# Encoder block on Trainium2: order and queues of the second MLP pass' operand loads, and place of the down passes' first operand

## The chip, the cores and the metric

One NeuronCore of a Trainium2 chip runs the whole program. The time is device microseconds of one execution; the kernel before is given by the median of three runs, and the profile is of one more execution.

## The reference

A transformer block over one sequence: 16 meta tokens are put ahead of the tokens, attention and a Fourier mix run side by side on one input projection, then comes an MLP with squared ReLU, and the final norm drops the meta tokens. All is float32. The change touches the MLP alone.

```python
D_MODEL = 1024; SEQ = 2048; DEPTH = 1; D_FF = 4 * D_MODEL
...
for i in range(DEPTH):
    hn = rms_norm(h, g_mix[i])
    proj = hn @ w_in[i]
    ...
    mixed = jnp.concatenate([rms_norm(attn, g_attn_out[i]), rms_norm(four, g_fourier_out[i])], axis=-1)
    h = h + mixed @ w_out[i]
    m = rms_norm(h, g_mlp[i])
    h = h + jnp.square(jax.nn.relu(m @ w_up[i])) @ w_down[i]
return rms_norm(h, g_final)[:, N_META:]
```

## The kernel before, in words

The MLP takes about the last 1,260 us of 2293 and runs in two passes (p = 0 and 1), each over 1024 tokens. A pass is `up_pass` (eight weight groups g of 512 columns of w_up) and then `down_pass` (four groups). Every product of two matrices is made in seven "forms" of Strassen's scheme, in the order `ORDER = "1265734"`; each form multiplies one sum or difference of quarter matrices by another and is added into one or two quarters of the result. Since the matrices are float32 and TensorE works on rounded parts, each operand is split into a high part (a cast on ScalarE, L70) and a low part (a subtraction on VectorE, L71), and `mm3` makes high x high (L80), high x low (L81) and low x high (L82). A form of the up pass is 24 matmuls, 12 for each half q; one of the down pass is 48, 12 for each token tile t, k = 0..3, where k = 0, 1 use the operand's half h = 0 and k = 2, 3 its half h = 1.

Names, which the profile's rows carry:

- `bf`: the activations' operand of an up form (2 MB, high and low part). For pass 1 all seven were worked out during pass 0 and lie in DRAM as `f_d`. Lines 1603 to 1612 make their tiles and load them: six in the pool `bfb`, form 7 in the tile `e0`. The tiles `e0` and `e1` (pool `ey`) hold residual rows `hs` (t = 0..3 and 4..7) while a down pass runs, and other things between.
- `R`: two raw tiles of 1 MB, w_up's 512 columns of one group. `up_weights` (L1119) makes from them the weight operands `wuh`, `wul` of the seven forms, with sums `us` on VectorE (L1138, L1139, L1142, L1144); there is a ring of three pairs of tiles (`wu_tile`, `WU_BUFS = 3`). Pass 1's first two weight operands are made in pass 0's down pass from their own loads `we` (L1413).
- `ux`, `uy`: PSUM results of up forms; `p` copies (L1246, ScalarE) and `c` sums (L1257, VectorE, then relu and square on ScalarE, L1212 and L1213) take them out; `keep` (L1219) writes c and their sums s to DRAM as `s_d`, which the down pass reads as `a`.
- `dx`, `dy`: PSUM results of down forms, added to `hs` on VectorE (L1485). The operands are `ah`, `al` (from `a`) and `bh`, `bl` (from `d`, w_down).
- Pass 0's last down group ends each token tile with the final norm: `ers` on GpSimd (L1444), scaling on VectorE (L1450) and ScalarE (L1451), and stores `out_dram<-hs` on GpSimd's queue (L1454).

Each engine, and SyncE (SP) as a DMA queue, runs its instructions strictly in the order in which they stand; an instruction that waits for a semaphore holds all behind it. The order on each engine comes from the order of the code's calls and a scheduler that moves DMAs ahead. Seven loads of pass 1's forms, R's loads and the writes `s_d` all stand on SP. `first_down` (L1279) loads and splits the down pass' first operand: `up_pass` steps it in its last group (L1237), where R's tiles are free, and it splits half h = 0, then h = 1, of a and b.

Of the kernel before, what the change touches and what calls it, by code (L numbers as in the profile page):

```python
# [11 lines left out]
F32 = mybir.dt.float32  # L12
R32 = mybir.dt.float32r
# [6 lines left out]
P = 128  # L20
# [32 lines left out]
ORDER = "1265734"  # L53
# [3 lines left out]
def f32v(ap):  # L57
    return ap.bitcast(F32)
# [26 lines left out]
def ins_of(x):  # L85
    return getattr(x, "ins", x)
# [49 lines left out]
def encoder_block(ctx: ExitStack, tc: tile.TileContext, x, meta, w_in, w_f,  # L136
                  w_out, w_up, w_down, g_fin, g_cols, g_rows, c_id, c_rope, c_dft, c_even, c_odd, c_rem, out):
    nc = tc.nc
    split = Split(nc)
    x = x[0]  # L140
    out = out[0]
    w_in, w_out, w_up, w_down, w_f = w_in[0], w_out[0], w_up[0], w_down[0], w_f[0]
# [9 lines left out]
    ey = Lines(ctx.enter_context(tc.tile_pool(name="ey", bufs=1)), small)  # L152
# [7 lines left out]
    wu = Lines(tc.alloc_tile_pool(name="wu", bufs=1, side="right"), small)  # L160
# [40 lines left out]
    f_d = {n: dram.tile([P, 2, 4, 512], F32, name=f"f_d{n}") for n in ORDER}  # L201
# [390 lines left out]
    for j in range(LAST + 1):  # L592
# [16 lines left out]
        else:  # L609
# [14 lines left out]
            a = 0  # L624
# [399 lines left out]
    for k in range(NQ):  # L1024
        for h in range(2):
            raw = a_tile(f"wor{k}_{h}")
# [77 lines left out]
    s_d = [dram.tile([P, 7, 4, 512], F32, name=f"s_d{g}") for g in range(4)]  # L1104
# [9 lines left out]
    def wu_tile(name, tag, shape=(4, 256)):  # L1114
        return wup.tile([P, *shape], R32, name=name, tag=tag, bufs=WU_BUFS)
# [34 lines left out]
    BT = {}  # L1150
# [14 lines left out]
    def forms_ahead():  # L1165

        area = u_tile("lf", 1).rearrange("p k n -> p (k n)")
        items = list(itertools.product(range(4), range(2)))
        r, turn = {}, [0]

        def load(k, i):
            for n, b, kk in (("11", 2, k), ("21", 2, k + 4), ("12", 3, k), ("22", 3, k + 4)):
                r[n] = area[:, 256 * len(r):256 * len(r) + 256] if n not in r else r[n]
                nc.sync.dma_start(r[n], m_d[b][:, kk, i * 256:i * 256 + 256])

        def keep(name, src, k, i):
            t = area[:, 1024 + 512 * turn[0]:1536 + 512 * turn[0]].rearrange("p (e n) -> p e n", e=2)
            turn[0] ^= 1
            split(t[:, 0].bitcast(R32), t[:, 1].bitcast(R32), src)
            nc.sync.dma_start(f_d[name][:, :, k, i * 256:i * 256 + 256], t)  # L1180

        sub = lambda d, a, b: nc.vector.tensor_tensor(r[d], r[a], r[b], op=ALU.subtract)
        load(*items[0])
        yield
        for at, it in enumerate(items):
            keep("1", r["11"], *it)
            keep("2", r["21"], *it)
            yield
            sub("11", "12", "11")
            keep("5", r["11"], *it)  # L1190
            yield
            sub("11", "22", "11")
            keep("6", r["11"], *it)
            yield
            sub("12", "22", "12")
            keep("7", r["12"], *it)
            yield
            keep("3", r["22"], *it)
            yield
            sub("21", "21", "11")  # L1200
            keep("4", r["21"], *it)
            if at + 1 < len(items):
                load(*items[at + 1])
            yield

    def up_pass(p, sp, pc, UW, ready, first, hs, beside):

        def c_tile(name):
            return pc.tile([P, 512], F32, name=f"{name}_{p}", tag="c", bufs=11)

        def relu2(dst, src):
            nc.scalar.activation(dst, src, AF.Relu)  # L1212
            nc.scalar.square(dst, dst)  # L1213

        for g in range(8):
            X, Y, p1, u2, p5, C = ({} for _ in range(6))

            def keep(name, q, t):
                nc.sync.dma_start(s_d[g // 2][:, ORDER.index(name), 2 * (g % 2) + q], t)  # L1219

            for name in ORDER:
                hi, lo = ready.pop(0)
                m = BF[name]
                for q in range(2):
                    if name == "1":
                        X[q] = bank(f"ux_{p}_{g}_{q}")
                    elif name in "25":
                        Y[q] = ybank(f"uy{name}_{p}_{g}_{q}")
                    o = (Y if name in "253" else X)[q]
                    ps = slice(q * P, (q + 1) * P)  # L1230
                    for k in range(4):
                        mm3(nc, o, (hi[:, k, ps], lo[:, k, ps]), (m[0][k], m[1][k]),
                            name in "125" and k == 0, k == 3, True)
                w = next(UW, None)
                if w is not None:
                    ready.append(w)
                elif g == 7:  # L1237
                    next(first, None)
                    if name == "7":
                        load_h(p, 0, hs)  # L1240
                for q in range(2):
                    nm = f"{g}_{q}"
                    if name in "165":
                        d = p1 if name == "1" else u2 if name == "6" else p5
                        d[q] = pc.tile([P, 512], F32, name=f"p{name}_{p}_{nm}", tag="p", bufs=P_BUFS)
                        nc.scalar.copy(d[q], (Y if name == "5" else X)[q])  # L1246
                    elif name == "4":
                        C["21", q] = c = c_tile("c21_" + nm)
                        relu2(c, X[q])
                        keep("2", q, c)  # L1250
                        s4 = c_tile("s4_" + nm)
                        nc.vector.tensor_tensor(s4, c, C["s2", q], op=ALU.subtract)
                        keep("3", q, s4)
                    else:
                        f, a, b = {"2": ("11", Y, p1), "7": ("22", X, p5), "3": ("12", Y, u2)}[name]
                        C[f, q] = c = c_tile(f"c{f}_{nm}")
                        nc.vector.tensor_tensor(c, a[q], b[q], op=ALU.add)  # L1257
                        relu2(c, c)
                        if name != "3":
                            keep("1" if name == "2" else "4", q, c)  # L1260
                        else:
                            s1, s2, s3 = (c_tile(f"s{i}_{nm}") for i in (1, 2, 3))
                            nc.vector.tensor_tensor(s1, c, C["22", q], op=ALU.add)
                            keep("5", q, s1)
                            nc.vector.tensor_tensor(s2, s1, C["11", q], op=ALU.subtract)
                            keep("6", q, s2)
                            C["s2", q] = s2
                            nc.vector.tensor_tensor(s3, C["11", q], c, op=ALU.subtract)
                            keep("7", q, s3)
                next(beside, None)  # L1270
        drain(first, beside)
# [4 lines left out]
            (nc.gpsimd if i else nc.sync).dma_start(HS[:, t], h_d[8 * p + 4 * i + t])  # L1276
            hs.append(HS[:, t])

    def first_down(p, spr, FIRST, sp):  # L1279

        a = spr.tile([P, 4, 512], F32, name=f"a1_{p}", tag="R0")
        nc.sync.dma_start(a, s_d[0][:, 0])
        w = spr.tile([P, 4, 512], F32, name=f"d11_{p}", tag="R1")
        for h in range(2):
            nc.sync.dma_start(w[:, 2 * h:2 * h + 2], w_down[h * 512:h * 512 + 256, :512].rearrange("(p r) d -> r p d", r=P))
        yield
        for h in range(2):
            for x, r in (("a", a), ("b", w)):
                tags = ("us1", "us2") if h and x == "b" else ("wuh", "wul")
                hi, lo = ((wu_tile(f"{x}{e}1_{p}_{h}", t, (2, 512)) if t[0] == "w" else  # L1290
                           sp.tile([P, 2, 512], R32, name=f"{x}{e}1_{p}_{h}", tag=t)) for e, t in zip("hl", tags))
                split(hi, lo, r[:, 2 * h:2 * h + 2])
                FIRST.append((hi, lo))
                yield

    def down_pass(p, sp, FIRST, hs):

# [248 lines left out]
    sp = right("sp0")  # L1546
    UW = up_weights(0, sp, sp)
    ready = [next(UW), next(UW)]
# [40 lines left out]
    rest = later_forms()  # L1589
    next(rest)  # L1590
    pc = right("pc0")
    hs, FIRST = [], []
    up_pass(0, sp, pc, UW, ready, first_down(0, sp, FIRST, sp), hs, itertools.chain(rest, forms_ahead()))
    pc.release()
    bu.release()
    bf2.release()
# [3 lines left out]
    spr = left("spr1")  # L1600
    UW = up_weights(1, sp, spr)
    bfb = left("bfb")
    for name in ORDER:
        if name == "7":
            bf_tile(ey, name, tag="e0")
        else:
            bf_tile(bfb, name)
    nc.sync.dma_start(f32v(BT["1"]), f_d["1"])
    nc.sync.dma_start(f32v(BT["2"]), f_d["2"])
    ready.append(next(UW))  # L1610
    for name in "65734":
        nc.sync.dma_start(f32v(BT[name]), f_d[name])
    pc = right("pc1")
    hs, FIRST = [], []
    up_pass(1, sp, pc, UW, ready, first_down(1, spr, FIRST, sp), hs, iter(()))
    pc.release()
    bfb.release()
    spr.release()
# [103 lines left out]
```

## Time and profile before

| | |
|---|---|
| median of three runs | 2296.43 us (2295.06 to 2297.25) |
| the profiled execution | 2295.14 us |
| its span, first to last instruction | 2293.4 us |
| mean granted clock of TensorE | 0.994 |
| TensorE (PE) busy | 2242.5 us, 98% |
| VectorE (DVE) busy | 1692.7 us, 74% |
| ScalarE (ACT) busy | 1177.4 us, 51% |
| GpSimd (POOL) busy | 247.2 us, 11% |
| DMA queue of SP and the other hardware queue, share of 16 engines | 39.9% |
| DMA queue of GpSimd | 7.7% |

TensorE is busy for nearly the whole span; its idle time is some 50 us, and a change gains only what it takes from that idle time or from stretches at a lower clock. A row of a timeline has the start and duration in us, engine, line, operation, what it writes and reads, the shapes, and in brackets how long the engine was idle before it and what ended the wait. Consecutive matmuls overlap, so their pace is read from starts, not from durations.

### The profile page before, as it was taken

To read this page: it belongs to the slowest core of one execution; us is meant where nothing else is said; L and a number is where in the kernel's file an instruction comes from. 1 tells how busy PE (TensorE), PEld (TensorE's weight loads), DVE (VectorE), ACT (ScalarE), POOL (GpSimd) and SP (SyncE) were. 2 spreads that over 40 slices of the span, in tenths; PEclk is the share of its full clock that TensorE was granted. 3 is DMA by queue.
4 is the path that set the end of the run, shared out by engine and by line. 5 is a ranking of instruction groups with operands and counts; after the bars stand their busy time and mean duration, and the time that the engine had idled before them with its cause. 6 is when DMAs were issued, how large, how long until landed. Compare 5 with 4: busy or idle time off the path is not lost.

```text
span 2293.4 us, 28136 instructions
## 1 busy us (share of the span) xinstructions
PE 2242.5 (98%) x10238; PEld 1775.1 (77%) x10238; DVE 1692.7 (74%) x2250; ACT 1177.4 (51%) x1997; POOL 247.2 (11%) x285
## 2 busy tenths in 40 slices
PE   9999999999999999999999999999789999899998
PEld 7888986766666666678888878888678888688887
DVE  6435589999998998887776579779555656596795
ACT  6443356656555666677555544334345555443343
POOL 2212120013222022010000010000200000100000
PEclk9999999999999999999999999999899999999999
DMA  6333252133343523366767675543574445764442
GB/s 204 87 105 87 66 164 71 51 120 100 115 137 120 204 87 119 123 262 234 237 227 234 235 276 176 172 129 119 198 302 151 154 149 187 299 201 158 129 138 83
DMA packets 191787, 367.41 MB, mean 160 GB/s; under 512 B 15760, under 2 KB 74768, under 8 KB 189984
## 3 DMA queue, kind: packets, MB, share of 16 engines
q1 hardware_dynamic: 171040, 310.08, 39.9%
q0 software_dynamic: 20464, 55.27, 7.7%
q8 instruction: 80, 1.31, 0.2%
q14 instruction: 59, 0.48, 0.1%
q10 hardware_dynamic: 144, 0.26, 0.0%
HBM read 236.28 MB, written 129.27 MB: 159 GB/s over the span
## 4 chain that ended last, share of the span: by engine, by line
PE 79%; DVE 8%; DMA 6%; ACT 3%; issue 2%; POOL 1%; SPq 1%; POOLq 0%; DVEq 0%; ACTq 0%
PE o L849 6%; PE dx L80 5%; PE dx L82 5%; PE dx L81 5%; PE dy L82 4%; PE dy L80 4%; PE dy L81 4%; PE ux L80 4%; PE ux L81 4%; PE ux L82 4%; PE uy L80 3%; PE uy L82 3%; PE uy L81 3%; PE s L80 2%; PE s L82 2%
## 5 line engine op out<-in xcount | busy, mean ns | idle before, releaser
L70 ACT CAST ah<-a 128x1024 fp32r<-128x1024 f32 x112 | 117.1, 1049 | 259.3 <-PE dx L81 104.9
L849 PE MATMUL o<-S,vn 128*128 128x512 f32 x512 | 243.6, 597 | 4.1 <-ACT S L841 3.4
L80 PE MATMUL dx<-bh,ah 128*128 128x512 f32 x512 | 199.3, 389 | 4.2 <-DVE hs L1485 2.5
L81 PE MATMUL dx<-bl,ah 128*128 128x512 f32 x512 | 199.1, 389 | 1.4 <-DVE bl L71 1.4
L82 PE MATMUL dx<-bh,al 128*128 128x512 f32 x512 | 199.2, 389 | 0.1
L80 PE MATMUL ux<-bf,wuh 128*128 128x512 f32 x448 | 176.8, 395 | 18.8 <-DMA bf<-f_d 18.7
L780 ACT COPY S<-s 128x512 f32<-128x512 f32 x256 | 145.0, 584 | 92.2 <-PE s L82 73.0
L81 PE MATMUL ux<-bf,wuh 128*128 128x512 f32 x448 | 175.8, 392 | 0.0
L82 PE MATMUL ux<-bf,wul 128*128 128x512 f32 x448 | 175.7, 392 | 0.0
L840 DVE TENSOR_TENSOR S<-S,mb 128x1024 f32<-128x1024 f32 x128 | 155.4, 1229 | 11.8 <-ACT mb L811 11.7
L841 ACT ACTIVATE S<-S 128x1024 f32<-128x1024 f32 x128 | 135.1, 1063 | 43.1 <-DVE S L840 41.9
L80 PE MATMUL dy<-bh,ah 128*128 128x512 f32 (+1 forms) x388 | 151.6, 391 | 4.9 <-ACT ah L70 4.9
L71 DVE TENSOR_TENSOR al<-a,ah 128x1024 fp32r<-128x1024 f32 x112 | 136.3, 1222 | 26.6 <-ACT ah L70 26.0
L82 PE MATMUL dy<-bh,al 128*128 128x512 f32 (+1 forms) x388 | 150.8, 390 | 0.7 <-DVE al L71 0.7
L81 PE MATMUL dy<-bl,ah 128*128 128x512 f32 (+1 forms) x388 | 151.3, 390 | 0.0
L849 PEld LDWEIGHTS o<-S,vn 128*128 128x128 f32 x512 | 92.2, 189 | 75.0 <-issue 59.0
L80 PE MATMUL s<-q,kt 128*128 128x512 f32 (+1 forms) x272 | 145.2, 534 | 2.7 <-ACT S L780 2.5
L71 DVE TENSOR_TENSOR bl<-d,bh 128x1024 fp32r<-128x1024 f32 x96 | 117.1, 1220 | 26.7 <-ACT bh L70 26.5
L80 PE MATMUL uy<-bf,wuh 128*128 128x512 f32 x320 | 125.2, 391 | 0.3 <-ACT wuh L70 0.3
L82 PE MATMUL uy<-bf,wul 128*128 128x512 f32 x320 | 124.7, 390 | 0.7 <-DVE wul L71 0.7
L81 PE MATMUL uy<-bf,wuh 128*128 128x512 f32 x320 | 124.9, 390 | 0.0
L786 DVE TENSOR_TENSOR M<-M,S 128x1024 f32<-128x1024 f32 x96 | 117.8, 1227 | 9.1 <-ACT S L780 8.1
(311 smaller groups left out, 5633.5 us busy)
## 6 DMA issues: line engine op xcount, KB each, us to landing
a<-s_d SPq DMA_DIRECT2D x84, 512.0 KB, 3.7
R<-in_w_up_dram SPq DMA_DIRECT2D x32, 1024.0 KB, 5.5
s_d<-s SPq DMA_DIRECT2D x128, 256.0 KB, 2.1
d<-in_w_down_dram SPq DMA_DIRECT2D x52, 512.0 KB, 5.1
s_d<-c SPq DMA_DIRECT2D x96, 256.0 KB, 2.8
f_d<-lf SPq DMA_DIRECT2D x56, 256.0 KB, 2.9
bf<-f_d SPq DMA_DIRECT2D x7, 2048.0 KB, 22.6
a<-s_d POOLq DMA_DIRECT2D x24, 512.0 KB, 5.6
```

Source lines behind the costliest of these rows:

```text
L70: self.high = nc.scalar.copy(hi, src)
L71: self.low = nc.vector.tensor_tensor(lo, src, f32v(hi), op=ALU.subtract)
L80: nc.tensor.matmul(out, a[0], b[0], start=first, stop=False, skip_group_check=chain)
L81: nc.tensor.matmul(out, a[0], b[1], start=False, stop=False, skip_group_check=chain)
L82: nc.tensor.matmul(out, a[1], b[0], start=False, stop=last, skip_group_check=chain)
L780: nc.scalar.copy(S[:, i % 2], ps)
L786: nc.vector.tensor_tensor(M, M, S, op=ALU.max)
L840: nc.vector.tensor_tensor(S, S, mb, op=ALU.subtract)
L841: nc.scalar.activation(p, S, AF.Exp, scale=ISQ)
L849: nc.tensor.matmul(s["O"], v[:, 2 * j % 4 + e], p[:, e], start=i + e == 1, stop=False)
```

## The change

Two things are changed. **The loads of pass 1's forms**: the six tiles of `bfb` are made in another order ("2165347"), so they lie on other parts of the memory that pass 0 leaves; form 7 is loaded from GpSimd's queue; and SP's loads are tied in the order form 1, form 2, R, forms 6, 5, 3, 4. **The first down operand**: its raw data goes into one tile `f1` in `e1` (a: 1 MB, w_down: twice 0.5 MB), loaded at a step of the sixth weight group (g = 5) where the scheduler may move it further ahead; half h = 1 of a is split into a tile of its own (R's place in pass 0, a new tag `fx` in pass 1), half h = 1 of b into `us1`, `us2`, and the halves h = 0 follow in two `wu` slots.

```diff
@@ -1234,6 +1234,8 @@
                 w = next(UW, None)
                 if w is not None:
                     ready.append(w)
+                    if (g, name) == (5, "1"):
+                        next(first)
                 elif g == 7:
                     next(first, None)
                     if name == "7":
@@ -1276,22 +1278,28 @@
             (nc.gpsimd if i else nc.sync).dma_start(HS[:, t], h_d[8 * p + 4 * i + t])
             hs.append(HS[:, t])
 
-    def first_down(p, spr, FIRST, sp):
-
-        a = spr.tile([P, 4, 512], F32, name=f"a1_{p}", tag="R0")
-        nc.sync.dma_start(a, s_d[0][:, 0])
-        w = spr.tile([P, 4, 512], F32, name=f"d11_{p}", tag="R1")
+    def first_down(p, FIRST, sp):
+
+        raw = ey.tile([P, 2, 4, 512], F32, name=f"f1_{p}", tag="e1")
+        nc.sync.dma_start(raw[:, 0], s_d[0][:, 0])
         for h in range(2):
-            nc.sync.dma_start(w[:, 2 * h:2 * h + 2], w_down[h * 512:h * 512 + 256, :512].rearrange("(p r) d -> r p d", r=P))
+            nc.sync.dma_start(raw[:, 1, 2 * h:2 * h + 2],
+                              w_down[h * 512:h * 512 + 256, :512].rearrange("(p r) d -> r p d", r=P))
+        FIRST += [None] * 4
         yield
-        for h in range(2):
-            for x, r in (("a", a), ("b", w)):
-                tags = ("us1", "us2") if h and x == "b" else ("wuh", "wul")
-                hi, lo = ((wu_tile(f"{x}{e}1_{p}_{h}", t, (2, 512)) if t[0] == "w" else
-                           sp.tile([P, 2, 512], R32, name=f"{x}{e}1_{p}_{h}", tag=t)) for e, t in zip("hl", tags))
-                split(hi, lo, r[:, 2 * h:2 * h + 2])
-                FIRST.append((hi, lo))
-                yield
+
+        def parts(i, hi, lo):
+            h, x = divmod(i, 2)
+            split(hi, lo, raw[:, x, 2 * h:2 * h + 2])
+            FIRST[i] = hi, lo
+
+        both = sp.tile([P, 4, 512], R32, name=f"a1p_{p}", tag="fx" if p else "R0")
+        parts(2, both[:, :2], both[:, 2:])
+        yield
+        parts(3, *(sp.tile([P, 2, 512], R32, name=f"b{e}1_{p}", tag=t) for e, t in (("h", "us1"), ("l", "us2"))))
+        for i in range(2):
+            parts(i, *(wu_tile(f"{'ab'[i]}{e}1_{p}", "wu" + e, (2, 512)) for e in "hl"))
+            yield
 
     def down_pass(p, sp, FIRST, hs):
 
@@ -1590,7 +1598,7 @@
     next(rest)
     pc = right("pc0")
     hs, FIRST = [], []
-    up_pass(0, sp, pc, UW, ready, first_down(0, sp, FIRST, sp), hs, itertools.chain(rest, forms_ahead()))
+    up_pass(0, sp, pc, UW, ready, first_down(0, FIRST, sp), hs, itertools.chain(rest, forms_ahead()))
     pc.release()
     bu.release()
     bf2.release()
@@ -1600,19 +1608,22 @@
     spr = left("spr1")
     UW = up_weights(1, sp, spr)
     bfb = left("bfb")
-    for name in ORDER:
+    for name in "2165347":
         if name == "7":
             bf_tile(ey, name, tag="e0")
         else:
             bf_tile(bfb, name)
-    nc.sync.dma_start(f32v(BT["1"]), f_d["1"])
-    nc.sync.dma_start(f32v(BT["2"]), f_d["2"])
-    ready.append(next(UW))
-    for name in "65734":
-        nc.sync.dma_start(f32v(BT[name]), f_d[name])
+    nc.gpsimd.dma_start(f32v(BT["7"]), f_d["7"])
+    behind = nc.sync.dma_start(f32v(BT["1"]), f_d["1"])
+    for name in "2U6534":
+        with tc.issue_after(ins_of(behind)):
+            if name == "U":
+                ready.append(next(UW))
+            else:
+                behind = nc.sync.dma_start(f32v(BT[name]), f_d[name])
     pc = right("pc1")
     hs, FIRST = [], []
-    up_pass(1, sp, pc, UW, ready, first_down(1, spr, FIRST, sp), hs, iter(()))
+    up_pass(1, sp, pc, UW, ready, first_down(1, FIRST, sp), hs, iter(()))
     pc.release()
     bfb.release()
     spr.release()
```

On SP's queue, at the end of pass 0, before: the `we` loads, then the forms' loads (`f_d_133` to `f_d_139` are forms 1, 2, 6, 5, 7, 3, 4; a name in brackets is a semaphore waited for, DMASW one of a GpSimd DMA, DMAHW one of another).

```order
L1413 DMA we_13878<-in_w_up_dram 128x4x256 [waits DMAHW3_49,DVE_49]
L1612 DMA bf_14104<-f_d_137 128x4096 [waits DMASW3_49,DMASW4_49,DMASW2_49,DMASW5_49,DMASW1_49,DMASW6_49,DMASW0_49,DMASW7_49,DVE_49,Activation_49]
L1608 DMA bf_14100<-f_d_133 128x4096 [waits DMAHW6_49,DMAHW7_49,DMAHW5_49,DMAHW4_49]
L1609 DMA bf_14101<-f_d_134 128x4096 [waits PE_49]
L1128 DMA R_1_0_14109<-in_w_up_dram 128x4x512
L1128 DMA R_1_0_14111<-in_w_up_dram 128x4x512
L1612 DMA bf_14102<-f_d_135 128x4096
L1612 DMA bf_14103<-f_d_136 128x4096 [waits PE_49]
L1612 DMA bf_14105<-f_d_138 128x4096 [waits PE_49]
L1612 DMA bf_14106<-f_d_139 128x4096 [waits DMAHW0_49,DVE_49,Activation_49]
```

The same place of the changed kernel:

```order
L1421 DMA we_13876<-in_w_up_dram 128x4x256 [waits DMAHW3_49,DVE_49]
L1617 DMA bf_14099<-f_d_133 128x4096 [waits PE_49]
L1623 DMA bf_14098<-f_d_134 128x4096 [waits DMAHW6_49,DMAHW5_49,DMAHW7_49,DMAHW4_49,DVE_49]
L1128 DMA R_1_0_14108<-in_w_up_dram 128x4x512
L1128 DMA R_1_0_14110<-in_w_up_dram 128x4x512
L1623 DMA bf_14100<-f_d_135 128x4096
L1623 DMA bf_14101<-f_d_136 128x4096 [waits PE_49]
L1623 DMA bf_14102<-f_d_138 128x4096 [waits PE_49]
L1623 DMA bf_14103<-f_d_139 128x4096 [waits DMASW0_49,DMASW7_49,DVE_49,Activation_49]
```

Form 7 (`f_d_137`) no longer stands at the head, form 1 does, and it waits for a matmul of pass 0's down pass that stands well ahead of the last form's; form 2 waits for the loads of the last a operand and their splits; form 5 waits for pass 0's last matmuls.

On GpSimd, in the final norm of pass 0 (`ers_5` is the one of token tile 5, the `hs_1` rows below it the stores of tiles 5 to 7), the changed kernel:

```order
L1462 DMA out_dram<-hs_1_11930 128x512 [waits DMASW0_49,Activation_49]
L1452 TENSOR_TENSOR ers_5_14039<-epm_5_11838,mhalf 128x1 [waits DVE_49,Pool_49]
L1616 DMA bf_14104<-f_d_137 128x4096 [waits DMASW4_49,DMASW5_49,DMASW3_49,DMASW6_49,DMASW2_49,DMASW1_49]
L1462 DMA out_dram<-hs_1_11930 128x512 [waits DVE_49]
L1462 DMA out_dram<-hs_1_11930 128x512 [waits Activation_49]
L1452 TENSOR_TENSOR ers_6_14060<-epm_6_11839,mhalf 128x1 [waits DVE_49,Pool_49]
L1452 TENSOR_TENSOR ers_7_14081<-epm_7_11840,mhalf 128x1 [waits DVE_49,Pool_49]
```

Before, the row of form 7 isn't there, and `ers_7` stands behind the stores of tile 6.

On VectorE, in the last weight group of pass 1, around form 3's results (`c_7_0`, `c_7_1` from `uy`), before:

```order
L71 TENSOR_TENSOR al_1_0_16328<-a_1_16283,ah_1_0_16327 128x1024 [waits DMAHW3_49,DVE_49,Activation_49]
L1257 TENSOR_TENSOR c_7_0_1_16331<-uy_1_7_0_16225,p_1_7_0_16221 128x512 [waits DMAHW0_49,PE_49]
L71 TENSOR_TENSOR bl_1_1_16404<-d_1_16285,bh_1_1_16403 128x1024 [waits DMAHW5_49,DVE_49,Activation_49]
L1263 TENSOR_TENSOR s_7_0_1_16335<-c_7_0_1_16331,c_7_0_1_16293 128x512 [waits DMAHW4_49,Activation_49]
L1265 TENSOR_TENSOR s_7_0_1_16336<-s_7_0_1_16335,c_7_0_1_16182 128x512 [waits DVE_49]
L1268 TENSOR_TENSOR s_7_0_1_16337<-c_7_0_1_16182,c_7_0_1_16331 128x512
L1257 TENSOR_TENSOR c_7_1_1_16344<-uy_1_7_1_16238,p_1_7_1_16223 128x512 [waits DMAHW6_49,PE_49]
L71 TENSOR_TENSOR bl_1_0_16382<-d_1_16285,bh_1_0_16381 128x1024 [waits DMAHW4_49,Activation_49]
```

The same place of the changed kernel:

```order
L71 TENSOR_TENSOR al_1_16332<-f_1_15577,ah_1_16331 128x1024 [waits Activation_49]
L1259 TENSOR_TENSOR c_7_0_1_16335<-uy_1_7_0_16227,p_1_7_0_16223 128x512 [waits DMAHW2_49,PE_49]
L1265 TENSOR_TENSOR s_7_0_1_16339<-c_7_0_1_16335,c_7_0_1_16293 128x512 [waits DMAHW6_49,Activation_49]
L1267 TENSOR_TENSOR s_7_0_1_16340<-s_7_0_1_16339,c_7_0_1_16184 128x512 [waits DMAHW5_49,DVE_49]
L1270 TENSOR_TENSOR s_7_0_1_16341<-c_7_0_1_16184,c_7_0_1_16335 128x512 [waits DMAHW7_49]
L1259 TENSOR_TENSOR c_7_1_1_16348<-uy_1_7_1_16240,p_1_7_1_16225 128x512 [waits DMAHW0_49,PE_49]
L71 TENSOR_TENSOR bl_1_16386<-f_1_15577,bh_1_16385 128x1024 [waits Activation_49]
```

The split of b's half h = 1 (`bl_1_1`) is gone from between c and s, and those that are left read `f_1` and wait for ScalarE's cast alone, not for a load.

## The prediction

> **What bounds the kernel now.** I read the costliest groups first, then who waits for whom on TensorE, then the timeline of the places found there. In the groups (idle time before a group stands behind the bar) one group of matmuls has far more idle time ahead of it than any other of the MLP, and the list of DMA issues has the loads that it waits for:
>
> ```profile
> L80 PE MATMUL ux<-bf,wuh 128*128 128x512 f32 x448 | 176.8, 395 | 18.8 <-DMA bf<-f_d 18.7
> bf<-f_d SPq DMA_DIRECT2D x7, 2048.0 KB, 22.6
> ```
>
> The waits of TensorE (total us, times, longest) agree; the second row is the next largest and belongs to the down passes:
>
> ```profile
> PE ux L80 <- DMA bf<-f_d: 18.7, 2, 12.6
> PE dy L80 <- ACT ah L70: 4.9, 2, 2.8
> ```
>
> The timeline of TensorE (start, duration, operation, and in brackets the wait) puts both DMA waits at the start of the second up pass:
>
> ```profile
> 1640.04 0.39 PE L80 MATMUL dx<-bh,ah 128*128 128x512 f32 x1
> ...
> 1644.57 0.39 PE L82 MATMUL dx<-bh,al 128*128 128x512 f32 x1
> 1657.58 0.77 PE L80 MATMUL ux<-bf,wuh 128*128 128x512 f32 x1 [12.62 <-DMA bf<-f_d]
> ...
> 1676.47 0.77 PE L80 MATMUL ux<-bf,wuh 128*128 128x512 f32 x1 [6.10 <-DMA bf<-f_d]
> ...
> 1681.23 0.40 PE L82 MATMUL ux<-bf,wul 128*128 128x512 f32 x1
> ```
>
> From 1640.04 to 1644.57 there are 20 steps, so TensorE's pace is 0.227 us a matmul, and a form of 24 matmuls takes 5.45 us. From the last dx (1644.57) to the row at 1681.23 there are 60 steps (forms 1 and 2, then 12 matmuls of form 6): 13.6 us at that pace, but 36.7 passed. **23.0 us** are lost there. They are more than the two waits, because matmuls behind a wait also ran slower. The loads were late for this reason (queue of SyncE, then its wait):
>
> ```profile
> 1613.11 2.65 SPq L1413 DMA_DIRECT2D we<-in_w_up_dram  x2
> 1642.47 0.34 SPq L1612 DMA_DIRECT2D bf<-f_d  x1
> 1642.97 0.34 SPq L1608 DMA_DIRECT2D bf<-f_d  x1
> 1643.36 0.45 SPq L1609 DMA_DIRECT2D bf<-f_d  x1
> 1643.86 1.59 SPq L1128 DMA_DIRECT2D R<-in_w_up_dram  x2
> 1645.49 19.63 SPq L1612 DMA_DIRECT2D bf<-f_d  x4
> ```
>
> ```profile
> SPq L1612 <- DMA out_dram<-hs: 26.4, 4, 23.0
> ```
>
> SyncE issues nothing between 1615.8 and 1642.5. At its head stands form 7's load, whose tile still holds output rows being stored; forms 1 and 2 are queued behind it though their tiles are free. Then seven loads of 2 MB and R's two of 1 MB share the DMA engines:
>
> ```profile
> 1643.90:1681.50 37.60, 18.89 (x66) 14.51 (x65) 12.50 (x15) 9.41 (x14) 4.51 (x9) 0.73 0.99 405
> 1643.60:1647.00 3.40, 1.36 (x7) 0.78 (x5) 1.76 (x4) 1.89 (x6) 2.01 (x4) 1.00 0.97 306
> 1647.00:1660.70 13.70, 3.12 (x8) 2.50 (x9) 1.32 (x3) 1.19 (x2) 2.81 (x5) 0.50 1.02 432
> 1984.90:1988.30 3.40, 1.84 (x9) 1.18 (x7) 0.67 (x1) 1.75 (x2) 0.00 (x0) 1.00 0.01 5
> 1988.30:1991.70 3.40, 2.16 (x9) 1.80 (x10) 3.40 (x4) 2.15 (x3) 0.27 (x1) 1.00 0.00 0
> ```
>
> In these windows (busy time of PE, PEld, DVE, ACT, POOL, then granted clock, DMA share, GB/s) the DMA engines are full at 405 GB/s, and the clock is at 0.50 after a stretch in which TensorE idled 2.0 of 3.4 us, but stays at 1.00 after one with 1.6 idle.
>
> **The forms' loads.** The new order puts form 1 at SyncE's head; it waits for a matmul of the first down pass some 25 us before the queue gets there, so it issues at 1615.8. Form 2 waits for the splits of the last a operand, the second of which is the 1625.04 row below, so it issues at 1626.4. R (two loads of 1 MB) and form 6 follow with no wait. From 1626.4 these are 6.3 MB, with about 2 MB of output stores beside them: 8.4 MB at 405 GB/s are 21 us, so all has landed by about 1647. Form 1 starts without a wait at 1644.8, form 2 at 1650.2. Both DMA waits go.
>
> What is late next is form 6's weight operand, which VectorE and ScalarE make from R and which stands on VectorE behind form 2's evacuations (c, L1257):
>
> ```profile
> 1625.04 1.22 DVE L71 TENSOR_TENSOR al<-a,ah 128x1024 fp32r<-128x1024 f32 x1
> ...
> 1671.52 1.23 DVE L1138 TENSOR_TENSOR us<-R,R 128x1024 f32<-128x1024 f32 x1 [3.08 <-DMA R<-in_w_up_dram]
> 1672.67 0.68 DVE L1257 TENSOR_TENSOR c<-uy,p 128x512 f32<-128x512 f32 x1
> 1673.27 1.22 DVE L1139 TENSOR_TENSOR us<-us,R 128x1024 f32<-128x1024 f32 x1
> 1674.52 1.23 DVE L1142 TENSOR_TENSOR R<-R 128x1024 f32<-128x1024 f32 x1
> 1675.66 2.35 DVE L71 TENSOR_TENSOR wul<-us,wuh 128x1024 fp32r<-128x1024 f32 x2
> ```
>
> ```profile
> 1674.58 1.97 ACT L70 CAST wuh<-us 128x1024 fp32r<-128x1024 f32 x2
> ```
>
> From the second c (1672.67) the cast starts 1.91 us later and one cast lasts 1.0; the first low part ends at 1675.66 + 1.2, 4.2 after c. In the changed kernel the order of these rows is the same, R has landed, and that c starts when form 2's second half ends, 1656.0. So form 6 starts at 1659.0 in place of 1655.7, a stall of 3.3; its third matmul (L82) waits for the low part until 1660.2, 0.7 more, and 0.2 are for slow first matmuls. Whether half clock follows depends on how the idle 4 us fall into stretches of 3.4: 2.0 idle was followed by it, 1.6 was not. I take one stretch of half clock: 3.4 us in which half, 1.7, is lost. The new loss is 3.3 + 0.7 + 0.2 + 1.7 = 5.9; bounds 4.2 (no half clock) and 7.6 (two stretches). The gain is 23.0 - 5.9 = **17.1 us**.
>
> Forms 5, 7, 3 and 4 are needed at 1664.5, 1669.9, 1675.4 and 1680.8. They are issued from 1643.9 on: 8.4 MB and 2 MB of stores at 405 GB/s are 26 us, all landed at 1670; forms 5 and 7, should they share evenly, after (4.2 + 1) / 0.405 = 13 us, at 1657. So they cost nothing with 7 us and more to spare. Form 7 from GpSimd finds its stores landed (SyncE saw that at 1642.47) and adds one issue, about half a microsecond, ahead of the last stores, which no engine waits for.
>
> Two queues do not make this faster. The Trainium skill, "DMA: Bandwidth & Descriptors", section "Issuing engines are not separate DMA queues", says that DMAs from any engine interleave on the same 16 engines and only the time to issue is saved; the trace's share of 0.99 agrees. By that page the GpSimd queue alone would be worth about the half microsecond of an issue, and the gain lies in what no longer stands behind form 7, which is how the sum counts it.
>
> **The first down operand.** Before, its raw data was loaded into R's tiles in the last weight group, so the splits came late (ScalarE, VectorE, TensorE):
>
> ```profile
> 1968.20 1.05 ACT L70 CAST bh<-d 128x1024 fp32r<-128x1024 f32 x1 [4.27 <-DMA d<-in_w_down_dram]
> ```
>
> ```profile
> 1969.29 1.23 DVE L71 TENSOR_TENSOR bl<-d,bh 128x1024 fp32r<-128x1024 f32 x1 [4.03 <-ACT bh L70]
> ```
>
> ```profile
> 1334.78 0.39 PE L82 MATMUL dx<-bh,al 128*128 128x512 f32 x1
> 1336.03 0.50 PE L80 MATMUL dx<-bh,ah 128*128 128x512 f32 x1 [0.85 <-ACT ah L70]
> ...
> 1974.29 0.50 PE L81 MATMUL dx<-bl,ah 128*128 128x512 f32 x1 [1.37 <-DVE bl L71]
> ...
> 1976.57 0.50 PE L80 MATMUL dx<-bh,ah 128*128 128x512 f32 x1 [0.85 <-ACT ah L70]
> ...
> 1989.54 0.50 PE L80 MATMUL dy<-bh,ah 128*128 128x512 f32 x1 [2.80 <-ACT ah L70]
> ```
>
> Now the data lands some 250 us ahead, and the half that is needed second is split long before; VectorE no longer stands 4.03 us behind a cast that waits for a DMA, so the b split that made 1.37 moves forward by about that. The wait of 0.85 cost 1.25 - 0.23 = 1.0 from start to start, 0.2 above itself, and the slow matmul behind it 0.1. Pass 0 gains **1.1**; pass 1, with 1.37 + 0.85 and twice 0.3, **2.8**. Form 2 of pass 1 waits for casts into the area of the first operand: they waited for matmul 47 of form 1's 48 and now wait for number 41, since the half read first now lies there: 6 x 0.227 = **1.4** of the 2.80. In pass 0 its place is unchanged and I count nothing. The early loads are 2 MB each pass, beside transfers with DMA share to spare; SyncE stands some 2 to 3 us at the load that waits for form 1's writes. Behind it is an R load with more slack than that. I count 0, bounds -1 and 3 us; -1 if DVE's forward move also shortens form 6's wait for the residual adds.
>
> **Sum.** 17.1 + 1.1 + 2.8 + 1.4 = 22.4. The profiled execution took 2295.1 (1.7 over its span), so 2272.7; the median of the runs is 1.3 above that execution, so I say **2274.0**.
>
> **Rivals.**
> *No half clock* behind the shorter waits: 1.7 less at form 6, and if the half clock that now stands behind the first pass' form 2 goes too, as the phase moves, 1.7 more: 2274.0 - 3.4 = 2270.6. For it: 4 us of idle fall into two stretches, and one with 1.6 idle did nothing. Against it: 2.0 was enough once. The Trainium skill, "TensorE: Matmul & The Clock Gate", section "Part 1: The HAM clock gate", has the clock fall after an idle window of about 3.4 us; by that rule this case holds, and the trace, where 2.0 idle of 3.4 sufficed, does not agree. Chance 0.13.
> *A wait takes the place:* form 7 on GpSimd's queue lands late. The stores of that queue are the nearest row:
>
> ```profile
> out_dram<-hs POOLq DMA_DIRECT2D x16, 256.0 KB, 4.3
> ```
>
> At 4.3 us per 256 KB, one behind another, 2 MB take 34 us: from 1643.9 to 1678, 8 late, and 2 of half clock: 2284. Chance 0.09.
> *Not what it says:* form 1's load still waits for the end of the down pass. It then issues near 1644, alone, and lands after 2.1 MB / 0.432 = 4.9 and some 2 us of start, 1651; 6 us and half clock for 3: 2283. Chance 0.06.
> *Slower than before:* the GpSimd load again, with its price beyond the whole gain. GpSimd works in order, so its last stores and the next loads stand behind; TensorE stops at form 7. It decides if the load lands later than 48 us after its issue (1669.9 + 22.4 is 1692): at 58 us the time is 2305 counted with half clock behind it. Nothing in the trace moves 2 MB so slowly (median 22.6 us with the engines full). Chance 0.04. For a gain lost without a loss I leave 0.04, and 0.64 for the forecast, 2271.5 to 2279.
>
> **Range** 2267 to 2285: down to the clock case less the 1 and the runs' spread, up past the two at 2283 and 2284; it leaves out the last two. A measurement here tells 0.2% (4.6 us) from no change. Faster 0.92, same 0.04, slower 0.04.
>
> **What the changed profile would show.** SyncE: form loads issued near 1616 and 1626. TensorE: no wait for f_d; a wait of about 3.3 for ScalarE's wuh ahead of form 6, and 0.7 for wul; from the last dx to form 6's twelfth matmul 19.5 us instead of 36.7. Down pass 1: no wait in form 1, about 1.4 in form 2. Wrong would be: a wait for f_d at forms 5 or 7, a ScalarE stop at the early cast in the second weight group, or stretches of half clock in places that had none.

## The result and the profile after

The changed kernel takes 2274.05 us (median of four runs, 2273.03 to 2276.69) beside 2296.81 before; the ratio is 0.9904, 95% interval 0.9887 to 0.9921. Run again on the chip of the later experiments it took 2276.24 beside 2294.69, ratio 0.9917 (0.9902 to 0.9932). So the two measured gains are 22.8 and 18.5 us; the forecast was 2274.0, by its sum a gain of 22.4. The sum came out, but not every term of it, as the trace shows. TensorE's waits after (total us, times, longest):

```profile
PE ux L80 <- ACT wuh L70: 6.8, 1, 6.8
PE dy L80 <- ACT ah L70: 3.5, 2, 2.1
```

Both waits for `f_d` are gone. In their place stands one wait at form 6 for its weight operand, twice as long as the forecast's 3.3. TensorE's timeline from the last dx to form 6's twelfth matmul:

```profile
1641.01 0.39 PE L82 MATMUL dx<-bh,al 128*128 128x512 f32 x1
...
1651.88 0.39 PE L82 MATMUL uy<-bf,wul 128*128 128x512 f32 x1
1659.06 0.79 PE L80 MATMUL ux<-bf,wuh 128*128 128x512 f32 x1 [6.79 <-ACT wuh L70]
...
1663.82 0.40 PE L82 MATMUL ux<-bf,wul 128*128 128x512 f32 x1
```

These 60 matmuls took 22.8 us; before it was 36.7, the forecast was 19.5. Why form 6's operand was late is seen on GpSimd, ScalarE and VectorE, in this order:

```profile
1638.67 1.12 POOL L1462 DMA_DIRECT2D out_dram<-hs  x2 [1.36 <-DVE epm L1447]
1639.80 0.57 POOL L1452 TENSOR_TENSOR ers<-epm,mhalf 128x1 f32<-128x1 f32 x1
1650.22 0.58 POOL L1616 DMA_DIRECT2D bf<-f_d  x1 [9.85 <-DMA out_dram<-hs]
1650.80 1.07 POOL L1462 DMA_DIRECT2D out_dram<-hs  x2
1651.88 1.08 POOL L1452 TENSOR_TENSOR ers<-epm,mhalf 128x1 f32<-128x1 f32 x2
```

```profile
1652.49 1.33 ACT L1459 ACTIVATE hs<-hs,ers 128x512 f32<-128x512 f32 x2 [9.55 <-POOL ers L1452]
1653.73 1.05 ACT L1248 COPY p<-ux 128x512 f32<-128x512 f32 x2
...
1657.98 1.98 ACT L70 CAST wuh<-us 128x1024 fp32r<-128x1024 f32 x2
```

```profile
1652.49 1.41 DVE L1458 SCALAR_TENSOR_TENSOR hs<-hs,ers,gf 128x512 f32<-128x512 f32 x2 [9.35 <-POOL ers L1452]
1654.32 0.69 DVE L1259 TENSOR_TENSOR c<-uy,p 128x512 f32<-128x512 f32 x1 [0.42 <-ACT p L1248]
1654.93 1.21 DVE L1138 TENSOR_TENSOR us<-R,R 128x1024 f32<-128x1024 f32 x1
1656.06 0.68 DVE L1259 TENSOR_TENSOR c<-uy,p 128x512 f32<-128x512 f32 x1
1656.66 1.21 DVE L1139 TENSOR_TENSOR us<-us,R 128x1024 f32<-128x1024 f32 x1
```

GpSimd stands 9.85 us at form 7's load, which waits for output stores. The last two `ers` are behind it; ScalarE waits 9.55 us for them, with the copies p behind that wait, and VectorE 9.35 us; VectorE's c then waits for p, the one that comes last, and the sums for form 6 stand behind c. The list of DMA issues (KB each, median us from issue to landing) shows that the stores landed late:

```profile
out_dram<-hs POOLq DMA_DIRECT2D x16, 256.0 KB, 13.8
```

The same row was 4.3 us before. Both medians mix stores that meet loads and stores that don't; of the first eight, which form 7's load waits for, one took 2.4 us in the median before and at most 2.6, and 6.8 and at most 13.5 after. SyncE's queue now issues its loads while the stores run, form 6's among them by the last row (four loads, which end with a wait):

```profile
1612.25 0.50 SPq L1617 DMA_DIRECT2D bf<-f_d  x1
1622.42 0.34 SPq L1623 DMA_DIRECT2D bf<-f_d  x1
1622.81 0.98 SPq L1128 DMA_DIRECT2D R<-in_w_up_dram  x2
1623.83 30.45 SPq L1623 DMA_DIRECT2D bf<-f_d  x4
```

In the second down pass form 1 no longer waits, form 2 waits for less, and the wait of form 6 for the residual adds is down too (the first row is that wait before, total, times and longest):

```profile
PE dx L80 <- DVE hs L1485: 2.5, 1, 2.5
```

```profile
1967.59 0.50 PE L80 MATMUL dy<-bh,ah 128*128 128x512 f32 x1 [1.45 <-ACT ah L70]
1969.23 0.50 PE L82 MATMUL dy<-bh,al 128*128 128x512 f32 x1 [0.91 <-DVE al L71]
1981.27 0.47 PE L80 MATMUL dx<-bh,ah 128*128 128x512 f32 x1 [1.30 <-DVE hs L1493]
```

By stretches (from the starts of the first and last matmuls in the two timelines; "repeat" is the changed kernel's profile on the later chip):

| stretch of TensorE | before | after | change | repeat | forecast of the change |
|---|---|---|---|---|---|
| start to first dx of pass 0 | 1333.5 | 1331.6 | -1.9 | 1333.4 | 0 |
| down pass 0 | 311.1 | 309.4 | -1.7 | 310.6 | -1.1 |
| last dx of pass 0 to first dx of pass 1 | 328.0 | 314.1 | -13.9 | 314.7 | -17.1 |
| down pass 1 | 313.7 | 309.2 | -4.5 | 309.2 | -4.2 |

### The profile page after: what moved, and what is told of

The parts are those of the page before. It is cut to its first block, busy times and chain, and to the rows that moved or that the text cites. A ratio compares the mean times of both kernels' runs of the same rounds, so it can differ in the third digit from the quotient of the medians.

```text
span 2271.2 us, 28115 instructions
## 1 busy us (share of the span) xinstructions
PE 2238.5 (99%) x10238; PEld 1772.9 (78%) x10238; DVE 1693.4 (75%) x2250; ACT 1178.0 (52%) x1997; POOL 245.6 (11%) x286
## 4 chain that ended last, share of the span: by engine, by line
PE 87%; DVE 6%; ACT 2%; issue 2%; POOL 1%; DMA 1%; SPq 0%; POOLq 0%; DVEq 0%; ACTq 0%
PE o L849 7%; PE ux L82 5%; PE ux L80 5%; PE ux L81 5%; PE dx L80 5%; PE dx L81 5%; PE dx L82 5%; PE uy L82 4%; PE uy L80 4%; PE uy L81 4%; PE dy L82 4%; PE dy L81 4%; PE dy L80 4%; PE s L80 2%; PE s L82 2%; PE s L81 2%
## 5 line engine op out<-in xcount | busy, mean ns | idle before, releaser
L80 PE MATMUL dx<-bh,ah 128*128 128x512 f32 x496 | 192.7, 388 | 1.3 <-DVE hs L1493 1.3
L82 PE MATMUL dx<-bh,al 128*128 128x512 f32 x496 | 192.6, 388 | 0.0
L81 PE MATMUL dx<-bl,ah 128*128 128x512 f32 x496 | 192.5, 388 | 0.0
L71 DVE TENSOR_TENSOR al<-a,ah 128x1024 fp32r<-128x1024 f32 x108 | 131.3, 1220 | 27.1 <-ACT ah L70 26.8
L71 DVE TENSOR_TENSOR bl<-d,bh 128x1024 fp32r<-128x1024 f32 x92 | 112.1, 1219 | 20.2 <-ACT bh L70 20.1
## 6 DMA issues: line engine op xcount, KB each, us to landing
bf<-f_d SPq DMA_DIRECT2D x6, 2048.0 KB, 13.6
```

The source lines that it names most:

```text
L71: self.low = nc.vector.tensor_tensor(lo, src, f32v(hi), op=ALU.subtract)
L80: nc.tensor.matmul(out, a[0], b[0], start=first, stop=False, skip_group_check=chain)
L81: nc.tensor.matmul(out, a[0], b[1], start=False, stop=False, skip_group_check=chain)
L82: nc.tensor.matmul(out, a[1], b[0], start=False, stop=last, skip_group_check=chain)
```

## The experiments

Each kernel is given by its difference from the changed kernel, unless it says otherwise. "Held" is GpSimd's wait at form 7's load.

**Form 7's load on SyncE.** Is it GpSimd that makes form 6 late?

```diff
-    nc.gpsimd.dma_start(f32v(BT["7"]), f_d["7"])
...
-    for name in "2U6534":
+    for name in "2U65734":
```

> The changed kernel with form 7's load on SyncE, between forms 5 and 3. Theory (GpSimd, held 9.85 us at form 7's load by stores that landed late, held the last two ers, with them ScalarE's scaling, the p copies and the c sums, and so form 6's operand): GpSimd no longer waits at a load, the c of form 2's first half comes near 1652 and not 1654.3, form 6 waits 3 to 4 us in place of 6.8, time 2270 to 2271.5 against 2274.0. Rival (form 6's operand is late because R and the sums share the DMA engines with the early loads): us waits for R, the wait at form 6 stays near 6.8, time 2274. Second rival (SyncE, held at form 7, now makes forms 3 and 4 late): a wait for f_d at form 7 or 3, time above 2276.

Measured 2272.45 us beside 2296.28, ratio 0.9902 (0.9887 to 0.9916). TensorE's timeline:

```profile
1641.10 0.39 PE L82 MATMUL dx<-bh,al 128*128 128x512 f32 x1
...
1655.48 0.50 PE L80 MATMUL ux<-bf,wuh 128*128 128x512 f32 x1 [3.11 <-ACT wuh L70]
...
1656.75 0.50 PE L82 MATMUL ux<-bf,wul 128*128 128x512 f32 x1 [0.54 <-DVE wul L71]
...
1660.00 0.63 PE L82 MATMUL ux<-bf,wul 128*128 128x512 f32 x1
```

```profile
1649.76 0.69 DVE L1259 TENSOR_TENSOR c<-uy,p 128x512 f32<-128x512 f32 x1 [2.91 <-PE uy L82]
```

With GpSimd free, c waits for TensorE and no longer for p, and the wait at form 6 is 3.1 us. The 60 matmuls take 18.9 us, 3.9 less than in the changed kernel; the prediction had 19.5. The store's median landing is still 12.2 us, but nothing that matters waits for a store now. The stretch gained only 2.1 us in all (312.0 against 314.1), since TensorE was still at half clock for about 1 us behind the 60 matmuls, and in the next weight group waited 0.69 us for a low part (at 1687.34). The time came out 1 us above the 2271.5 that was expected at most, and in the medians of the runs the two kernels can't be told apart; it is the trace that decides.

**Form 7's load on GpSimd, behind the last ers.**

```diff
-    nc.gpsimd.dma_start(f32v(BT["7"]), f_d["7"])
...
+    with tc.issue_after(POWS[-1]):
+        nc.gpsimd.dma_start(f32v(BT["7"]), f_d["7"])
```

`POWS` lists the `ers` instructions in their order.

> The changed kernel with form 7's load still on GpSimd, but behind the last ers. Theory (only the place on GpSimd matters): as with the load on SyncE, form 6 waits 3 to 4 us, 2270 to 2271.5. Rival (the load on GpSimd's own queue slows its stores or its ers wherever it stands): 2273 or more, and GpSimd still waits between the stores.

Measured 2275.51 beside 2296.28, ratio 0.9917 (0.9903 to 0.9932), a time such as the rival's. GpSimd does still wait between stores, as the rival has it, but no `ers` stands behind that wait any more, and form 6 is not later for it. TensorE's waits and GpSimd's row say where it went:

```profile
1656.66 0.50 PE L80 MATMUL ux<-bf,wuh 128*128 128x512 f32 x1 [3.11 <-ACT wuh L70]
...
1672.93 0.47 PE L80 MATMUL ux<-bf,wuh 128*128 128x512 f32 x1 [2.86 <-DMA bf<-f_d]
```

```profile
1650.29 0.58 POOL L1618 DMA_DIRECT2D bf<-f_d  x1 [3.05 <-DMA out_dram<-hs]
```

Form 6's wait is the 3.1 us of the theory. But the load still waits for stores, is issued at 1650.3, and comes 2.9 us too late for form 7: the prediction's rival of a late form 7, at a third of its price. Behind the same stores the load is no earlier for standing on a queue of its own.

**Only the loads**, with the first down operand as before (its lines of the diff undone).

> The loads of the forms as changed, the first down operand as before. If the two parts add up, by the traces' stretches (13.9 us in the second up pass, 6.2 in the two down passes): about 2296.6 - 13.9 = 2282 to 2283, with the waits 0.85, 1.37 and 2.80 of the down passes back. Rival (the first operand's early loads cost the second up pass something, by DMA or by SyncE): the second up pass gains more than 13.9 here, 2280 or less.

Measured 2281.93 beside 2296.28, ratio 0.9945 (0.9928 to 0.9962). The waits:

```profile
PE ux L80 <- ACT wuh L70: 6.6, 1, 6.6
PE dy L80 <- ACT ah L70: 4.9, 2, 2.8
...
PE dx L81 <- DVE bl L71: 1.8, 2, 1.2
...
PE dx L80 <- ACT ah L70: 1.7, 2, 0.9
```

The second up pass takes 313.6 us as in the changed kernel, and the down passes' waits are back (311.8 and 313.5). GpSimd is held 9.6 us.

**Only the first down operand**, with the loads as before (their lines undone).

> The first down operand as changed, the forms' loads as before. If the parts add up: 2296.6 - 6.2 = 2290 to 2291, the two waits for f_d (18.7 us) as before, no wait in form 1 of the down passes. By the sum of the prediction 1.1 + 2.8 + 1.4 = 5.3: 2291.3. Rival (the raw tile in e1 or the loads ahead cost elsewhere): 2293 or more.

Measured 2289.40 beside 2296.28, ratio 0.9971 (0.9961 to 0.9982):

```profile
PE ux L80 <- DMA bf<-f_d: 18.8, 2, 12.9
PE dy L80 <- ACT ah L70: 3.5, 2, 2.1
```

The waits for `f_d` are whole, the down passes take 309.4 and 309.2 us. The two parts, 14.4 and 6.9 us, add up to 21.2, beside 22.8 and 18.5 measured for both together: no interaction shows within the spread of the runs, and no cost of the first operand's early loads.

**Form 6's operand ahead of form 2's sums**, on top of form 7's load on SyncE.

```diff
+                        with tc.issue_after(LOW6[0]) if p and g == 0 and name == "2" else nullcontext():
+                            nc.vector.tensor_tensor(c, a[q], b[q], op=ALU.add)
...
                 ready.append(next(UW))
+                LOW6[:] = [ins_of(split.low)]
```

> Form 7's load on SyncE, and in the first group of the second up pass the c sums of form 2 stand behind form 6's low part, so form 6's operand is made while form 1 runs. Theory (what is left at form 6 is the order on VectorE, behind the c sums): no wait at form 6, the 60 matmuls from the last dx on take 14 to 15 us and not 18.9 as with form 7's load on SyncE alone, time 2267 to 2269. Rival (R or the us tiles are not free before, or the p copies hold form 6): a wait of 2 us or more stays at form 6, 2271 to 2273. Second rival (c, now later, keeps TensorE from the next banks or delays form 5's and 7's operands): the wait moves to forms 5 to 4, 2271 or more.

Measured 2266.75 beside 2294.69, ratio 0.9878 (0.9863 to 0.9893); the changed kernel had 0.9917 (0.9902 to 0.9932) on the same chip. TensorE:

```profile
1642.33 0.39 PE L82 MATMUL dx<-bh,al 128*128 128x512 f32 x1
...
1655.93 0.39 PE L82 MATMUL ux<-bf,wul 128*128 128x512 f32 x1
```

```profile
1647.96 1.22 DVE L1138 TENSOR_TENSOR us<-R,R 128x1024 f32<-128x1024 f32 x1
1649.21 1.23 DVE L1139 TENSOR_TENSOR us<-us,R 128x1024 f32<-128x1024 f32 x1
```

The 60 matmuls take 13.6 us, their bare pace, where 14 to 15 were expected: all 23.0 us that were lost there are back. The operand's sums start at 1648, as form 2 starts. It is the fastest of the kernels tried.

**Only form 7 moved**: places of the six tiles and SyncE's order as before, without ties; the first down operand as changed.

```diff
-    for name in "2165347":
+    for name in ORDER:
...
-    behind = nc.sync.dma_start(f32v(BT["1"]), f_d["1"])
-    for name in "2U6534":
...
+    nc.sync.dma_start(f32v(BT["1"]), f_d["1"])
+    nc.sync.dma_start(f32v(BT["2"]), f_d["2"])
+    ready.append(next(UW))
+    for name in "6534":
+        nc.sync.dma_start(f32v(BT[name]), f_d[name])
```

> Of the loads' part only form 7's move to GpSimd's queue is left: the six tiles lie where they lay before and nothing ties SyncE's order; the first down operand as changed. Theory (what counts is that form 7 no longer stands ahead of forms 1 and 2): form 1 is issued near 1622.5 and not 1612, lands ten us ahead of its use, time as the changed kernel, 2273 to 2275. Rival (the places are what frees forms 1 and 2 early enough): a wait for f_d at form 1 or 2, 2276 to 2282.

Measured 2272.77 beside 2294.69, ratio 0.9903 (0.9886 to 0.9919): not slower than the changed kernel on the same chip. Form 1 is issued at 1623.5 and is in time. The places and the ties are therefore not what gains here. The wait at form 6 is there too, but with another cause, since form 6's own load lands later and GpSimd is held less:

```profile
1658.84 0.76 PE L80 MATMUL ux<-bf,wuh 128*128 128x512 f32 x1 [5.46 <-DMA bf<-f_d]
```

```profile
1645.41 0.58 POOL L1616 DMA_DIRECT2D bf<-f_d  x1 [3.94 <-DMA out_dram<-hs]
```

So the places and the ties do bring form 6's load in earlier: with them, in the kernel with form 6's operand ahead, form 6 started at 1653.4 and did not wait for it. That they are needed once the operand is early is likely, but no run shows that kernel without them.

**Form 6's load later**, behind form 5's on SyncE: does the hold come from the early loads?

```diff
-    for name in "2U6534":
+    for name in "2U5634":
```

> The changed kernel with form 6's load behind form 5's on SyncE, so that it is issued near 1641 and not near 1624; form 7 stays on GpSimd. Theory (the early loads of form 6 and the others fill the DMA engines, so GpSimd's stores land late and hold GpSimd at form 7): less than half of the hold of 9.85 us is left, 0 to 4 us, and a store takes under 10 us and not 13.8; form 6 may wait for its own load until 1652 to 1659. Rival (the hold has another cause, such as the queue's order or the stores' own pace): the hold stays 8 to 10 us.

Measured 2274.91 us, a single run. GpSimd's row and the stores:

```profile
1642.50 0.58 POOL L1616 DMA_DIRECT2D bf<-f_d  x1 [1.55 <-DMA out_dram<-hs]
```

```profile
out_dram<-hs POOLq DMA_DIRECT2D x16, 256.0 KB, 6.7
```

Without form 6's 2 MB among the early loads the hold falls from 9.85 to 1.55 us and a store lands in 6.7 us. So in this trace the hold goes with the early loads, and with form 6's above all. In this kernel's order form 5 runs ahead of form 6, and TensorE waits 4.1 us for form 5's operand, the second cast of the same chain behind c; nothing is gained in time:

```profile
1656.93 0.50 PE L80 MATMUL uy<-bf,wuh 128*128 128x512 f32 x1 [4.06 <-ACT wuh L70]
```

**The changed kernel again.**

> The changed kernel once more, beside the others on their chip: 2273 to 2276, with GpSimd held 8 to 11 us at form 7's load and 6 to 7.5 us of waiting at form 6.

Measured 2276.24 beside 2294.69. GpSimd is held 9.35 us and form 6 waits 6.3:

```profile
PE ux L80 <- ACT wuh L70: 6.3, 1, 6.3
```

Both the hold and the wait came again. What did not come again is the shorter stretch ahead of the first dx: 1333.4 us here, 1331.6 in the first profile, and 1333.5 before.

## Why the prediction was right, point by point

*What bounds it, and what removes it*: right. Form 7 at SyncE's head held forms 1 and 2; with only form 7 moved, the time is that of the whole change. The prediction gave SyncE's new order the credit; for form 1 the ties and the places only bring its load another ten us ahead of a use that was already in time, and form 6's earlier load is of no use while its weight operand is late. None of its signs of being wrong came: no wait for `f_d` at forms 5 or 7, no stop of ScalarE before the early cast (it starts at 1711.70 straight behind a copy), and no half clock in a new place.

*What is late next*: right in kind. Form 6 waits for the chain behind c on VectorE, as the kernel with form 7 on SyncE shows, at 3.1 us against 3.3 forecast and 18.9 for the 60 matmuls against 19.5, and as the kernel with the chain ahead shows by having no wait at all.

*The step that was wrong*: "Form 7 from GpSimd finds its stores landed (SyncE saw that at 1642.47) and adds one issue". That landing was read off a trace in which no load ran beside the stores. The same prediction counted 2 MB of stores among the transfers that fill the engines until 1647, and did not carry this to the instruction that waits for the stores. The hold was 9.85 us, the new loss at form 6 was 22.8 - 13.6 = 9.2 us and not 5.9, and the up pass gained 13.9 and not 17.1. "Which no engine waits for" looked at the last stores and not at the last two `ers`, which stand behind form 7's load as well, as the rows of GpSimd's order given with the change already have it: ScalarE and VectorE wait for those.

*Half clock*: counted as one stretch of 3.4 us, 1.7 lost. In the changed kernel half clock stood there; two windows (PE, PEld, DVE, ACT, POOL busy, clock, DMA share, GB/s):

```profile
1656.90:1660.30 3.40, 1.22 (x2) 0.50 (x2) 3.37 (x4) 3.37 (x5) 0.00 (x0) 0.50 1.03 439
1660.30:1663.70 3.40, 3.38 (x9) 2.73 (x10) 3.38 (x3) 0.60 (x1) 0.00 (x0) 0.57 0.98 420
```

It lasted nearly through both, longer than counted, but the first row is mostly wait. Form 6's first twelve matmuls took 1663.82 - 1659.06 = 4.8 us from first to last start in place of 2.5, so the low part, the slow start and half clock together cost 2.3 where 0.7 + 0.2 + 1.7 = 2.6 was counted. What was mis-sized is the stall alone, 3.3 counted and 1659.06 - 1651.88 - 0.23 = 6.95 measured. The rival without half clock did not come about. The prediction's bracket, half clock behind 2.0 us of idle time in 3.4 and none behind 1.6, is no sharp rule either: in the kernel with form 7 on SyncE a window with 1.66 idle (1964.87 to 1968.28) was followed by a clock of 0.50, and one with 1.88 (1650.84 to 1654.25) by 1.00.

*The first down operand*: forecast 1.1 + 2.8 + 1.4 = 5.3; by itself it gained 6.9 us in the medians and 6.3 in the two stretches. Form 1's waits are gone. Form 2's wait of 2.80 fell to 1.45, the forecast 1.4, but a wait of 0.91 for its low part is new; in return the wait for the residual adds fell from 2.51 to 1.30, which stood in the prediction as a bound of 1 us and not in the sum.

*Why the sum agrees*: the up pass gained 3.2 less than forecast; the down passes gained 0.9 more, and 1.9 came from the stretch ahead of them. That 1.9 is no gain of the change: the repeat does not show it (1333.4), and the kernel with only the loads, whose code is as before there, has 1331.4. Without it the terms add up to 13.9 + 6.2 = 20.1 us, and in the repeat to 13.3 + 0.5 + 4.5 = 18.3. So the agreement of the sum is in part luck: a term that was 3.2 too large was made up by others and by the spread of the runs.

## What to carry to other kernels

An in-order queue that mixes transfers with small instructions that another engine waits for is a bad place for a load that waits: the load's wait becomes that engine's. When loads are moved ahead, whatever else moves data in the same stretch can get slower, as the stores did here, so a landing time from the trace of before holds only for what the move doesn't crowd. And when a wait is removed, the operand chain behind it should be moved with it: here that took the 60 matmuls from 18.9 to 13.6 us, 5.3, where the mishap cost 3.9.

## What was not expected of the hardware

How the two queues share the DMA engines. The list of queues (packets, MB, share of 16 engines) of the changed kernel between 1641 and 1650, while GpSimd was held:

```profile
q1 hardware_dynamic: 208, 3.13, 81.5%
q0 software_dynamic: 207, 0.68, 18.7%
```

SyncE's queue (q1) and GpSimd's (q0) got nearly the same number of packets, 208 and 207; but a packet of a form's load has 3.13 MB / 208 = 15 KB in the mean and one of a store 0.68 / 207 = 3.3 KB, so the stores got under a fifth of the time. The kernel with only form 7 moved, between 1638 and 1645, when R's loads stood in SyncE's queue:

```profile
q0 software_dynamic: 518, 1.71, 60.0%
q1 hardware_dynamic: 604, 1.20, 44.1%
```

R's packets have 2 KB (1.20 MB / 604), and the stores beside them moved 1.71 MB in 7 us, 0.244 MB per us against 0.076 in the rows above. GpSimd was held only 3.94 us there although more loads were still to land. By these two windows what slowed the stores is the size of the other queue's packets, not the number of bytes that were queued; no run changes the packet size alone. The Trainium skill, "DMA: Bandwidth & Descriptors", section "SWDGE vs HWDGE vs iDMA", says that inside each DMA engine the two kinds of queues are served in turn; the packet counts agree, 208 to 207 in the first window and 316 to 310 in the first four us of the second, while over all 7 us of it GpSimd's queue got fewer (518 to 604).
